# The down projection of a gated FFN: ten of its 21 blocks of rows go in pairs through seven products of blocks in place of eight

## The chip, the cores and the metric

The kernel runs on one core of one Trainium2 chip. The metric is the device time of one execution in microseconds (us), of which smaller is better; several executions are timed, and one more is profiled.

## The reference

One decoder layer for 512 tokens of 1024 channels in float32: a token mixer (pooling and sparse attention) and then an FFN. Only the FFN matters here; `D_FF` is 2752 and the convolution has three taps.

```
def conv_ffn(h, w_up, conv_w, conv_b, w_down):
    u = h @ w_up                                   # (512, 1024) @ (1024, 5504)
    up = jnp.pad(u, ((0, 0), (CONV_WIDTH - 1, 0), (0, 0)))
    c = conv_b + conv_w[0] * up[:, 0:S]
    for tap in range(1, CONV_WIDTH):
        c = c + conv_w[tap] * up[:, tap:tap + S]
    gate, val = jnp.split(c, 2, axis=-1)
    return (jax.nn.silu(gate) * val) @ w_down      # (512, 2752) @ (2752, 1024)

h = rms_norm(x, ffn_norm_w[l])
x = x + conv_ffn(h, w_up[l], conv_w[l], conv_b[l], w_down[l])
```

## The kernel before

Everything lies transposed: channels on the 128 partitions, the 512 tokens along the free dimension. Each float32 operand of a product is split in two numbers of TensorE's format, `hi` and `lo` (the rest), and a product of two blocks is three matmuls: hi by hi, lo of the one by hi of the other, and the reverse (`mm3`, lines 105 to 111). ScalarE (ACT) writes `hi`, VectorE (DVE) then writes `lo` (`split`, lines 93 to 103).

Weights come through a ring (`Ring`, lines 148 to 164). SyncE (SP) issues one load for up to 1024 columns into one of two staging tiles `st`, and the load waits until DVE has written the `lo` of the staging tile's earlier content. ACT and DVE then split it into tiles of up to 512 columns, `hi` and `lo`, of which there are six each; a `split` waits until TensorE (PE) is through with the tile six back.

The FFN has two stages. The up projection makes 43 tiles of 128 channels (`conv_tile`, lines 831 to 839): 24 matmuls of 512 columns each, then the scaling by `rstdb`, the convolution on DVE and ACT, and for each pair of a gate and a value tile the product silu(gate) * value, which is split into `gh[j]` and `gl[j]`, j from 0 to 20. The last 64 of the 2752 rows stand in `gs`, high part on partitions 0 to 63 and low part on 64 to 127, so that two matmuls do their product.

The down projection (lines 859 to 880) goes over the eight blocks c of 128 output channels. For each there are three loads of 7 weight blocks (448 KB), 21 times three matmuls with the 512 tokens moving, two matmuls for `gs`, one addition of the residual `x1[c]` on DVE from PSUM, and the store. The eighth block is done in two halves of 256 tokens with a PSUM bank each. That is 7 x 65 matmuls of 512 columns and 130 of 256.

The order of the instructions on each engine is set by a scheduler when the kernel is built: the code gives the program's order, and the scheduler may put independent instructions of one engine in another order. On the chip each engine takes its own queue in order. PSUM has eight banks: six under the tag `m` and two under `g`.

Of the kernel before, what the change touches and what calls it, by code (L numbers as in the profile page):

```python
# [11 lines left out]
F32 = mybir.dt.float32  # L12
# [7 lines left out]
P = 128  # L20
S = 512
# [49 lines left out]
START = ((2, 2, 2, 2), (1, 1, 1, 1))  # L71
SS = (0, 0, 0, 0)
ST = (1, 1, 1)


@with_exitstack
def layer(ctx: ExitStack, tc: tile.TileContext, par, masks, xT, w_kva, w_tm, w_fm, w_pl, w_pbr,
          w_ab, w_o, w_up, w_dn, w_dl, cw1, cw2, outT):
    nc = tc.nc
    v, a, g, pe = nc.vector, nc.scalar, nc.gpsimd, nc.tensor  # L80
    cnt = [0]
# [49 lines left out]
    def bank(p, tag, name, bufs):  # L131
        return p.tile([P, S], F32, tag=tag, name=nm(name), bufs=bufs)
# [686 lines left out]


    fp = pool(ctx, "fp")
    gh = [fp.tile([P, S], F32R, name=f"gh{j}") for j in range(NG - 1)]
    gl = [fp.tile([P, S], F32R, name=f"gl{j}") for j in range(NG - 1)]
    gs = fp.tile([P, S], F32R, name="gs")
    wlh = fp.tile([P, 1024], F32R, name="wlh")
    wll = fp.tile([P, 1024], F32R, name="wll")
    conv = fp.tile([P, NFT, 4], F32, name="conv")
    nc.sync.dma_start(conv, par[:, NCONV:].rearrange("p (t c) -> p t c", c=4))

    def conv_tile(t):  # L830
# [6 lines left out]
        v.scalar_tensor_tensor(c[:, 2:], u[:, :S - 2], conv[:, t, 0:1], c[:, 2:], ALU.mult, ALU.add)  # L837
        return c

    for j in range(NG):  # L840
# [10 lines left out]
        a.activation(cg[:rows], cg[:rows], AF.Silu)  # L851
        v.tensor_tensor(cg[:rows], cg[:rows], cv[:rows], ALU.mult)
        if j == 0:
            split(gs[:64], gs[64:], cg[:64])
        else:
            split(gh[j - 1], gl[j - 1], cg)

    wls = wr.tile([P, 1024], F32, tag="st", name="wls", bufs=ring.bufs[0])
    for h in range(2):
        nc.sync.dma_start(wls[64 * h:64 * h + 64], w_dl)  # L860
    split(wlh, wll, wls)
    for c in range(8):
        sl = slice(c * P, (c + 1) * P)

        cols = [slice(0, S)] if c < 7 else [slice(h * S // 2, (h + 1) * S // 2) for h in range(2)]
        banks = [bank(psm, "m", "dn", 6) for _ in cols]
        ws = []
        for q_ in range(3):
            ws += ring(w_dn[c, :, q_ * 896:(q_ + 1) * 896], P, 7)
            if q_ < 2:  # L870
                for ps, cs in zip(banks, cols):
                    mm3(ps[:, cs], [(ws[k], (gh[k][:, cs], gl[k][:, cs])) for k in range(7 * q_, 7 * q_ + 7)],
                        first=q_ == 0, last=False)
        for ps, cs in zip(banks, cols):
            mm3(ps[:, cs], [(ws[k], (gh[k][:, cs], gl[k][:, cs])) for k in range(14, 21)], first=False, last=False)
            pe.matmul(ps[:, cs], wlh[:, sl], gs[:, cs], start=False, stop=False)
            pe.matmul(ps[:, cs], wll[:, sl], gs[:, cs], start=False, stop=True)
            o = fp.tile([P, S], F32, tag="o", name=nm("o"), bufs=2)
            v.tensor_tensor(o[:, cs], ps[:, cs], x1[c][:, cs], ALU.add)
            nc.sync.dma_start(outT[sl, cs], o[:, cs])  # L880


def _tables():
# [28 lines left out]
def _layout(inp):  # L912
# [18 lines left out]
    for j in range(21):  # L931
# [5 lines left out]

    w_in = one("w_in")
    dn = one("w_down")
    d = {  # L940
        "par": par,
        "masks": _masks(),
# [9 lines left out]
        "w_dn": tiles(dn[:2688]),  # L952
        "w_dl": dn[2688:],
        "cw1": np.stack([kmaj(w) for w in one("cmp_w1")]),
        "cw2": one("cmp_w2"),
    }
# [16 lines left out]
```

## Time and profile before

| | us |
|---|---|
| three timed runs | 836.55, 837.82, 837.59 |
| their median | 837.59 |
| the profiled execution, its time | 835.79 |
| its span, first to last instruction | 834.0 |
| first matmul of the down projection | 712.00 |
| last matmul of the down projection | 830.60 |

Of the profiled execution 1.8 us lie outside the span that the trace shows, and the median of the runs is 1.8 us above it.

A line of the trace names the program's line, the engine, the operation and the tiles (out<-in). `dn` is a PSUM bank of the down projection, `fm` one of the up projection. PEld is TensorE's weight load; a row of PE or PEld is longer than the distance between two of them, since they overlap in a pipeline.

### The profile page before, as it was taken

What the parts mean: (1) busy time and instruction counts of PE and PEld (TensorE: products, weight loads), DVE (VectorE), ACT (ScalarE), POOL (GpSimd) and SP (SyncE); (2) the same over time, 40 slices, a digit from 0 to 9 for tenths busy, and PEclk for the clock granted to TensorE, in tenths of its full rate; (3) what the DMA queues carried; (4) which work ended last, traced back from release to release, by engine and by line L of the source; (5) the groups of instructions that cost most, each with busy time, mean ns of one, the idle gap of its engine ahead of it and who ended that gap; (6) DMA issues with size and microseconds to landing.
All of it is one profiled execution on the core that took longest, in us unless ns stands there. A gap on an engine that the chain in (4) does not pass through costs nothing.

```text
span 834.0 us, 12146 instructions
## 1 busy us (share of the span) xinstructions
PE 814.9 (98%) x4291; PEld 694.2 (83%) x4291; DVE 558.1 (67%) x1178; ACT 457.2 (55%) x977; POOL 226.7 (27%) x308
## 2 busy tenths in 40 slices
PE   7999989999999999999999999999999999999998
PEld 6878979987878878788888888888888888888888
DVE  7598865778887878885555438877777776532321
ACT  6755766668777877884334436554544544322220
POOL 5687514357565765641001200000000000000000
PEclk9999999999999999999999999999999999999999
DMA  6443362550001100011443233322333333343430
GB/s 219 116 114 113 104 176 86 169 152 26 26 26 41 36 26 26 26 51 51 152 152 97 84 101 95 105 84 97 101 101 102 89 90 115 99 126 101 115 101 26
DMA packets 29861, 77.55 MB, mean 93 GB/s; under 512 B 5480, under 2 KB 10216, under 8 KB 29800
## 3 DMA queue, kind: packets, MB, share of 16 engines
q1 hardware_dynamic: 29800, 76.78, 30.7%
q8 instruction: 34, 0.56, 0.3%
q14 instruction: 27, 0.22, 0.1%
HBM read 69.94 MB, written 2.10 MB: 86 GB/s over the span
## 4 chain that ended last, share of the span: by engine, by line
PE 85%; DVE 8%; ACT 3%; POOL 2%; DMA 1%; issue 1%; SPq 0%; DVEq 0%; ACTq 0%; POOLq 0%
PE fm L111 16%; PE fm L110 16%; PE fm L109 16%; PE op L735 5%; PE dn L110 5%; PE dn L109 5%; PE dn L111 5%; PE tp L728 4%; PE ss L698 2%; PE ss L697 2%; PE tg L321 2%; PE tg L320 2%; PE tg L319 2%; PE pb L109 1%; PE pb L110 1%
## 5 line engine op out<-in xcount | busy, mean ns | idle before, releaser
L97 ACT ACTIVATE hi<-st 128x512 fp32r<-128x512 f32 (+3 forms) x253 | 151.8, 607 | 192.5 <-PE fm L110 91.1
L100 DVE TENSOR_TENSOR lo<-st,hi 128x512 fp32r<-128x512 f32 (+1 forms) x210 | 142.6, 683 | 108.5 <-ACT hi L97 107.4
L109 PE MATMUL fm<-h2h,hi 128*128 128x512 f32 x344 | 133.9, 389 | 0.0
L110 PE MATMUL fm<-h2l,hi 128*128 128x512 f32 x344 | 133.8, 389 | 0.0
L111 PE MATMUL fm<-h2h,lo 128*128 128x512 f32 x344 | 133.7, 389 | 0.0
L709 POOL TENSOR_TENSOR pb<-pb,sm 128x128 f32<-128x128 f32 (+3 forms) x128 | 91.3, 745 | 51.1 <-DVE sm L706 28.0
L687 ACT ACTIVATE pb<-pb,nm 128x384 f32<-128x384 f32 (+3 forms) x128 | 70.9, 554 | 11.9 <-DVE nm L686 10.9
L109 PEld LDWEIGHTS fm<-h2h,hi 128*128 128x128 f32 x344 | 64.6, 188 | 13.5
L110 PEld LDWEIGHTS fm<-h2l,hi 128*128 128x128 f32 x344 | 64.6, 188 | 13.3
L111 PEld LDWEIGHTS fm<-h2h,lo 128*128 128x128 f32 x344 | 64.6, 188 | 13.3
L109 PE MATMUL fm<-hh,hi 128*128 128x512 f32 x160 | 71.1, 444 | 0.0
L111 PE MATMUL dn<-gh,lo 128*128 128x512 f32 (+1 forms) x189 | 69.1, 365 | 0.0
L110 PE MATMUL dn<-gl,hi 128*128 128x512 f32 (+1 forms) x189 | 69.1, 365 | 0.0
L109 PE MATMUL dn<-gh,hi 128*128 128x512 f32 (+1 forms) x189 | 69.1, 365 | 0.0
L686 DVE CUSTOM_DVE_ANT_0 pb<-ss,mk 128x384 f32<-128x384 f32 (+3 forms) x128 | 58.8, 485 | 14.5 <-PE ss L698 10.2
L111 PE MATMUL fm<-hh,lo 128*128 128x512 f32 x160 | 63.3, 396 | 0.7 <-POOL lo L100 0.7
L100 DVE TENSOR_TENSOR ptl<-tp,pth 128x512 fp32r<-128x512 f32 (+1 forms) x96 | 56.6, 594 | 10.8 <-ACT pth L97 10.3
L110 PE MATMUL fm<-hl,hi 128*128 128x512 f32 x160 | 63.0, 394 | 0.0
L97 ACT ACTIVATE pth<-tp 128x512 fp32r<-128x512 f32 (+1 forms) x96 | 49.3, 517 | 24.3 <-PE tp L728 24.1
L100 POOL TENSOR_TENSOR lo<-st,hi 128x512 fp32r<-128x512 f32 x36 | 47.8, 1333 | 37.5 <-ACT hi L97 32.6
L319 PE MATMUL tg<-hi,hh 128*128 128x256 f32 x192 | 54.1, 285 | 0.0
L320 PE MATMUL tg<-hi,hl 128*128 128x256 f32 x192 | 54.0, 285 | 0.0
(256 smaller groups left out, 1788.8 us busy)
## 6 DMA issues: line engine op xcount, KB each, us to landing
st<-in_w_up SPq DMA_DIRECT2D x43, 512.0 KB, 3.5
st<-in_w_dn SPq DMA_DIRECT2D x24, 448.0 KB, 3.7
st<-in_w_fm SPq DMA_DIRECT2D x20, 512.0 KB, 3.5
st<-in_w_tm SPq DMA_DIRECT2D x12, 512.0 KB, 3.6
qp<-qs SPq DMA_DIRECT2D x32, 128.0 KB, 2.6
st<-in_w_ab SPq DMA_DIRECT2D x8, 512.0 KB, 3.5
st<-in_w_o SPq DMA_DIRECT2D x8, 512.0 KB, 3.5
x<-in_xT SPq DMA_DIRECT2D x15, 256.0 KB, 5.1
```

The costliest lines, as they stand in the source:

```text
L97: a.activation(hi, src, AF.Copy)
L100: (eng or v).tensor_tensor(lo, src, r32(hi), ALU.subtract)
L109: pe.matmul(ps, sh, mh_, start=first and i == 0, stop=False)
L110: pe.matmul(ps, sh, ml_, start=False, stop=False)
L111: pe.matmul(ps, sl, mh_, start=False, stop=last and i == n - 1)
L319: pe.matmul(ps[:, :n], hh[k][:, tt], H, start=k == 0, stop=False)
L320: pe.matmul(ps[:, :n], hl[k][:, tt], H, start=False, stop=False)
L686: v.tensor_tensor_reduce(p_, ps, mcaus[:, S - n:], -1.0, 3e38, ALU.add, ALU.min, nm_[:, i:i + 1])
L687: a.activation(p_, p_, AF.Exp, bias=nm_[:, i:i + 1], scale=-1.0, accum_out=sm[:, i:i + 1])
L709: g.tensor_tensor(pb[:, PBASE[i]:PBASE[i] + n], pb[:, PBASE[i]:PBASE[i] + n], sm[:, i:i + 1].to_broadcast([P, n]), ALU.mult)
L728: last = pe.transpose(tp[:, n:n + P], pb[:, PBASE[i] + j * P:PBASE[i] + (j + 1) * P], ident)
L735: pe.matmul(op[:, j * P:], V2[b][j][:, G], pt_[:, TBASE[j]:TBASE[j] + w], start=b == 0 and j == 0 and part == 0, stop=False)
```

## The change

The last 11 blocks of rows and the 64 rows at the end stay as they were. The first ten go in five pairs p. The output channels go in four groups m of two blocks, so that a pair and a group have four weight blocks, and the tokens go in two halves of 256. The 2 x 2 x 2 products of blocks with 256 columns are replaced by seven products (the form of Strassen's scheme that is due to Winograd): sums of the activations are made in the up projection (`sums`), sums of the weights when they are loaded (`weights7`), and the seven products accumulate over the five pairs in four banks, of which `bb` and `bd` also take the 11 ordinary blocks.

- Activations: for a pair, the two products silu * value stand in `R` (128 x 1024). GpSimd (POOL) makes four differences of 128x256 in `T`, and ACT and DVE split 768 columns of `R` and the 1024 of `T` into `Bh[p]`, `Bl[p]`. For the last eight blocks the product is kept unsplit in `gw`, and its split is made in group 0 of the down projection, into the tiles of `h2h` and `h2l`, which are free after the last matmul of the up projection.
- Weights: a load of four blocks (256 KB) into `raw`, one of two staging tiles under the tag `rw`; one difference on POOL (line 906), three sums on DVE (lines 907 to 909), each 128x128; splits of 512 and of 384 columns through the ring's tiles. The ordinary blocks come in loads of 256 KB through the ring.
- In a group the steps alternate: c0 (an ordinary block for both output blocks, six matmuls of 512 columns), s0 (a pair, 21 matmuls of 256 columns), c1, s1, and so on to s4, then c5 to c11.
- After s4 the partial sums of `ba` and `bc` are combined on ACT and DVE and added to the residual; after c11 `bb` and `bd` are added, and `x1` itself is stored. In group 3 the second block's addition and store go in two halves.

```diff
+NSP = 5
+    NCB = NG - 1 - 2 * NSP
+    NEB = NCB - KC
+    def sums(jb, cg, cv):
+        if jb % 2 == 0:
+            raws[0] = [fp.tile([P, 4, 256], F32, tag="rw", name=nm("rw"), bufs=2) for _ in range(2)]
+        R, T = raws[0]
+        e = 2 * (jb % 2)
+        v.tensor_tensor(R[:, e:e + 2].rearrange("p k c -> p (k c)"), cg, cv, ALU.mult)
+        if jb % 2:
+            p = jb // 2
+            g.tensor_tensor(T[:, 0], R[:, 0], R[:, 1], ALU.subtract)
+            g.tensor_tensor(T[:, 1], R[:, 2], R[:, 0], ALU.subtract)
+            g.tensor_tensor(T[:, 2], R[:, 2], T[:, 0], ALU.subtract)
+            g.tensor_tensor(T[:, 3], R[:, 3], T[:, 2], ALU.subtract)
+            split(Bh[p][:, :3], Bl[p][:, :3], R[:, 1:4])
+            split(Bh[p][:, 3:], Bl[p][:, 3:], T)
...
+    def m256(ps, sa, k, p, first, done):
+        for n_, (w_, b_) in enumerate(((0, Bh), (0, Bl), (1, Bh))):
+            last = pe.matmul(ps, sa[w_], b_[p][:, k], start=first and n_ == 0, stop=done and n_ == 2)
+        return last
+    def weights7(m, p):
+        raw = fp.tile([P, 8, P], F32, tag="rw", name=nm("raw"), bufs=2)
+        nc.sync.dma_start(raw[:, 0:4], w_ds[m, p].rearrange("p (k c) -> p k c", c=P))
+        g.tensor_tensor(raw[:, 4], raw[:, 1], raw[:, 0], ALU.subtract)
+        v.tensor_tensor(raw[:, 5], raw[:, 0], raw[:, 3], ALU.add)
+        v.tensor_tensor(raw[:, 6], raw[:, 3], raw[:, 4], ALU.subtract)
+        v.tensor_tensor(raw[:, 7], raw[:, 2], raw[:, 6], ALU.subtract)
+        res = []
+        for o, n in ((1, 4), (5, 3)):
+            hi, lo = (wr.tile([P, 512], F32R, tag=t_, name=nm(t_), bufs=ring.bufs[1])[:, :n * P]
+                      .rearrange("p (k c) -> p k c", c=P) for t_ in ("hi", "lo"))
+            split(hi, lo, raw[:, o:o + n])
+            res += [(hi[:, k], lo[:, k]) for k in range(n)]
+        return res
...
-    for c in range(8):
...
-                    mm3(ps[:, cs], [(ws[k], (gh[k][:, cs], gl[k][:, cs])) for k in range(7 * q_, 7 * q_ + 7)],
...
+    for m in range(4):
...
+        for kind, i in order:
+            if kind == "c":
+                if m == 0 and NEB <= i < NCB:
+                    split(gh[i], gl[i], gw[i - NEB])
+                if i % 2 == 0:
+                    n = min(2, NCB + 1 - i)
+                    cload = ring(w_dc[m, :, i * 256:(i + n) * 256], P, 2 * n)
...
+            A11, A12, A22, S3, S1, S2, S4 = weights7(m, i)
+            for ps, hf, A, k, new in ((ba, 0, A11, 0, True), (bb, 1, A12, 2, False), (bd, 1, A22, 6, False),
+                                      (bc, 1, S3, 4, True), (bc, 0, S1, 3, False), (ba, 1, S2, 5, False),
+                                      (bb, 0, S4, 1, False)):
...
+        for e, (ps, x_) in enumerate(((bb, x1a), (bd, x1b))):
+            c = 2 * m + e
+            for cs in H if end and e else [slice(0, S)]:
+                v.tensor_tensor(x_[:, cs], ps[:, cs], x_[:, cs], ALU.add)
+                nc.sync.dma_start(outT[c * P:(c + 1) * P, cs], x_[:, cs])
```

Up to the first matmul of the down projection the queue of PE is the same in both kernels. In the down projection PE had, for a block of rows, three matmuls of 512 columns with the weights moving on by one block each time (here the first output block of those that follow the first two):

```order
L109 MATMUL dn_7895<-gh_5792,hi_7898 128x512
L110 MATMUL dn_7895<-gl_5813,hi_7898 128x512
L111 MATMUL dn_7895<-gh_5792,lo_7899 128x512
L109 MATMUL dn_7895<-gh_5793,hi_7898 128x512
L110 MATMUL dn_7895<-gl_5814,hi_7898 128x512
```

Now it has, at the end of c4 and the start of s4 in group 1 (`dn_8018` to `dn_8021` are bb, bd, ba, bc of that group; `hi_8216`, `lo_8217` are the first four weight blocks of s4):

```order
L940 MATMUL dn_8019<-gh_7689,hi_8200 128x512
L940 MATMUL dn_8019<-gl_7690,hi_8200 128x512
L940 MATMUL dn_8019<-gh_7689,lo_8201 128x512
L899 MATMUL dn_8020<-Bh_5812,hi_8216 128x256
L899 MATMUL dn_8020<-Bl_5817,hi_8216 128x256
L899 MATMUL dn_8020<-Bh_5812,lo_8217 128x256
```

Each product of a pair is three matmuls of 256 columns, and the third needs the `lo` that DVE writes.

DVE's queue in the down projection was low parts of weights in the order of their use, with one addition for each output block:

```order
L100 TENSOR_TENSOR lo_7831<-st_7828,hi_7830 128x512
L100 TENSOR_TENSOR lo_7835<-st_7828,hi_7834 128x384
L100 TENSOR_TENSOR lo_7862<-st_7859,hi_7861 128x512
L100 TENSOR_TENSOR lo_7866<-st_7859,hi_7865 128x384
L879 TENSOR_TENSOR o_7793<-dn_7697,x_0_5404 128x512
L100 TENSOR_TENSOR lo_7899<-st_7896,hi_7898 128x512
```

Now DVE has, in the middle of group 1 (`raw_8122`, `raw_8163` and `raw_8210` hold the weights of s2, s3 and s4 of this group, `raw_8333` those of s0 of the next):

```order
L101 TENSOR_TENSOR lo_8129<-raw_8122,hi_8128 128x512
L101 TENSOR_TENSOR lo_8133<-raw_8122,hi_8132 128x384
L101 TENSOR_TENSOR lo_8170<-raw_8163,hi_8169 128x512
L907 TENSOR_TENSOR raw_8210<-raw_8210 128x128
L101 TENSOR_TENSOR lo_8174<-raw_8163,hi_8173 128x384
L908 TENSOR_TENSOR raw_8210<-raw_8210 128x128
L909 TENSOR_TENSOR raw_8210<-raw_8210 128x128
L101 TENSOR_TENSOR lo_8201<-st_8198,hi_8200 128x512
L907 TENSOR_TENSOR raw_8333<-raw_8333 128x128
L908 TENSOR_TENSOR raw_8333<-raw_8333 128x128
L909 TENSOR_TENSOR raw_8333<-raw_8333 128x128
L101 TENSOR_TENSOR lo_8217<-raw_8210,hi_8216 128x512
```

The sums of a later load stand ahead of the low parts of an earlier one: the three sums on `raw_8333` ahead of `lo_8217` of s4.

SP's queue had three loads and a store for each output block:

```order
L155 DMA st_8057<-in_w_dn 128x896
L155 DMA st_8094<-in_w_dn 128x896
L155 DMA st_8125<-in_w_dn 128x896
L880 DMA out<-o_7991 128x512
L155 DMA st_8156<-in_w_dn 128x896
```

Now it has, in the same part of group 1, the loads of both kinds and the two stores of group 0:

```order
L905 DMA raw_8122<-in_w_ds 128x512
L905 DMA raw_8163<-in_w_ds 128x512
L970 DMA out<-x_0_5404 128x512
L970 DMA out<-x_1_5405 128x512
L156 DMA st_8261<-in_w_dc 128x512
L905 DMA raw_8210<-in_w_ds 128x512
L905 DMA raw_8333<-in_w_ds 128x512
L156 DMA st_8279<-in_w_dc 128x512
```

A load into `raw` waits until DVE has written the second low part (384 columns) of the load two back, and whatever stands behind it in SP's queue waits with it.

## Rows read from the trace of the kernel before

**Rows 1.** The page's first part: busy us of each engine, share, instructions.
```profile
PE 814.9 (98%) x4291; PEld 694.2 (83%) x4291; DVE 558.1 (67%) x1178; ACT 457.2 (55%) x977; POOL 226.7 (27%) x308
```

**Rows 2.** Busy time by stage: end of up, and down projection (PEclk: granted TensorE clock).
```profile
core 0: us, PE busy (x) PEld busy (x) DVE busy (x) ACT busy (x) POOL busy (x), PEclk, DMA share, GB/s
600.00:712.00 112.00, 112.00 (x496) 92.75 (x495) 83.20 (x124) 54.98 (x83) 0.00 (x0) 1.00 0.34 98
712.00:834.00 122.00, 118.88 (x586) 100.97 (x584) 35.56 (x58) 26.51 (x46) 0.00 (x0) 1.00 0.33 96
```

**Rows 3.** The chain of work that ended last, 712 to 834, by line.
```profile
by line: PE dn L110 31.4%; PE dn L109 31.4%; PE dn L111 31.4%; PE dn L877 1.5%; PE dn L876 1.5%; DVE o L879 0.3%; PE fm L111 0.2%; issue 0.0%
```

**Rows 4.** Who waited for whom, 720 to 834: us in total, times, longest.
```profile
ACT hi L97 <- PE dn L110: 74.3, 40, 2.6
```

**Rows 5.** Timeline: the down projection's first and last matmuls, last addition, last store.
```profile
712.00 0.39 PE L109 MATMUL dn<-gh,hi 128*128 128x512 f32 x1
...
815.13 0.28 PE L109 MATMUL dn<-gh,hi 128*128 128x256 f32 x1
...
830.60 0.28 PE L877 MATMUL dn<-gs,wll 128*128 128x256 f32 x1
830.92 0.42 DVE L879 TENSOR_TENSOR o<-dn,x 128x256 f32<-128x256 f32 x1 [2.33 <-PE dn L877]
831.37 0.33 SPq L880 DMA_DIRECT2D out<-o  x1
```

**Rows 6.** Groups by form, 720 to 834: busy us, mean ns | idle before.
```profile
L109 PEld LDWEIGHTS dn<-gh,hi 128*128 128x128 f32 x177 | 33.4, 189 | 5.3
...
L100 DVE TENSOR_TENSOR lo<-st,hi 128x512 fp32r<-128x512 f32 x20 | 13.9, 693 | 43.9 <-ACT hi L97 43.9
L97 ACT ACTIVATE hi<-st 128x512 fp32r<-128x512 f32 x20 | 12.6, 632 | 46.1 <-PE dn L110 46.1
...
L100 DVE TENSOR_TENSOR lo<-st,hi 128x384 fp32r<-128x384 f32 x20 | 11.2, 558 | 24.7 <-ACT hi L97 24.7
```

**Rows 7.** Groups by form, whole span: the small additions and POOL's.
```profile
L686 DVE CUSTOM_DVE_ANT_0 pb<-ss,mk 128x128 f32<-128x128 f32 x32 | 9.1, 286 | 4.2 <-PE tp L728 2.7 <-DMA qp<-qs 0.8
...
L300 POOL TENSOR_TENSOR h<-h,T 128x128 f32<-128x128 f32 x32 | 16.4, 533 | 47.0 <-issue 30.7 <-ACT h L293 15.1 <-DVE hrs L305 0.8
...
L100 POOL TENSOR_TENSOR hi<-st,hi 128x256 fp32r<-128x256 f32 x8 | 6.8, 848 | 4.7 <-ACT hi L97 4.7
```

**Rows 8.** DMA issues (KB each, us to landing) at 713.5 and at 428.7, and their starts.
```profile
st<-in_w_dn SPq DMA_DIRECT2D x1, 448.0 KB, 3.2
...
st<-in_w_o SPq DMA_DIRECT2D x1, 512.0 KB, 3.5
x<-in_xT SPq DMA_DIRECT2D x1, 256.0 KB, 3.6
...
428.72 0.33 SPq L155 DMA_DIRECT2D st<-in_w_o  x1
429.32 0.33 SPq L810 DMA_DIRECT2D x<-in_xT  x1
```

**Rows 9.** Timeline: POOL behind ACT at 445; DVE behind PE at 449.
```profile
445.07 0.62 ACT L212 ACTIVATE sq<-x 128x512 f32<-128x512 f32 x1
445.82 1.29 POOL L213 TENSOR_TENSOR ssum<-ssum,sq 128x512 f32<-128x512 f32 x1 [66.88 <-ACT sq L212]
...
448.73 0.39 PE L111 MATMUL fm<-mh,lo 128*128 128x512 f32 x1
...
449.16 0.69 DVE L813 TENSOR_TENSOR x<-fm,x 128x512 f32<-128x512 f32 x1 [1.49 <-PE fm L111]
```

**Rows 10.** Timeline from 21.4: DVE and POOL at work at the same time.
```profile
21.47 1.56 DVE L100 TENSOR_TENSOR lo<-st,hi 128x512 fp32r<-128x512 f32 x2 [0.42 <-ACT hi L97]
...
21.59 1.77 POOL L277 TENSOR_TENSOR C<-pl__110 128x128 f32<-128x128 f32 x2
```

More of the change, by code (lines that the diff above doesn't have):

```diff
@@ L821, in layer @@
     fp = pool(ctx, "fp")
[L822 to L823 removed]
+    NCB = NG - 1 - 2 * NSP
+    NEB = NCB - KC
+    gh = [fp.tile([P, S], F32R, name=f"gh{j}") for j in range(NEB)]
+    gl = [fp.tile([P, S], F32R, name=f"gl{j}") for j in range(NEB)]
+    gw = [fp.tile([P, S], F32, name=f"gw{j}") for j in range(KC)]
     gs = fp.tile([P, S], F32R, name="gs")
[L825 to L826 removed]
+    fp.tile([P, 48], F32, name="fpad")
+    Bh = [fp.tile([P, 7, 256], F32R, name=f"Bh{p}") for p in range(NSP)]
+    Bl = [fp.tile([P, 7, 256], F32R, name=f"Bl{p}") for p in range(NSP)]
     conv = fp.tile([P, NFT, 4], F32, name="conv")
@@ L851, in layer @@
         a.activation(cg[:rows], cg[:rows], AF.Silu)
+        if j and j <= 2 * NSP:
+            sums(j - 1, cg, cv)
+            continue
+        k = j - 1 - 2 * NSP
+        if j and k >= NEB:
+            v.tensor_tensor(gw[k - NEB], cg, cv, ALU.mult)
+            continue
         v.tensor_tensor(cg[:rows], cg[:rows], cv[:rows], ALU.mult)
@@ L855, in layer @@
         else:
[L856 to L861, printed above, removed]
-    for c in range(8):
[L863 to L871, printed above, removed]
-                    mm3(ps[:, cs], [(ws[k], (gh[k][:, cs], gl[k][:, cs])) for k in range(7 * q_, 7 * q_ + 7)],
[L873 to L880, printed above, removed]
@@ new lines, in layer @@
+            split(gh[k], gl[k], cg)
+    for k in range(KC):
+        gh.append(xp.tile([P, S], F32R, tag=f"hh{k}", name=f"gh{NEB + k}"))
+        gl.append(xp.tile([P, S], F32R, tag=f"hl{k}", name=f"gl{NEB + k}"))
+    def m256(ps, sa, k, p, first, done):
[16 more added lines that the diff above has]
+        return res
@@ L939, in _layout @@
     dn = one("w_down")
+    blk = lambda k, c: dn[k * P:(k + 1) * P, c * P:(c + 1) * P]
+    ds = np.stack([np.stack([np.concatenate([blk(2 * p, 2 * m + 1), blk(2 * p, 2 * m), blk(2 * p + 1, 2 * m),
+                                             blk(2 * p + 1, 2 * m + 1)], axis=1) for p in range(NSP)])
+                   for m in range(4)])
+    rem = np.concatenate([dn[2688:], dn[2688:]])
+    dc = np.stack([np.concatenate([blk(k, c) for k in range(2 * NSP, 21) for c in (2 * m, 2 * m + 1)]
+                                  + [rem[:, 2 * m * P:(2 * m + 2) * P]], axis=1) for m in range(4)])
     d = {
@@ L951, in _layout @@
         "w_up": tiles(one("w_up")[:, cols]),
-        "w_dn": tiles(dn[:2688]),
-        "w_dl": dn[2688:],
+        "w_ds": ds,
+        "w_dc": dc,
         "cw1": np.stack([kmaj(w) for w in one("cmp_w1")]),
```

36 lines of the change are left out of this document (35 added, 1 removed).

## The prediction

> **What bounds the kernel now.** I read the page's first part to find the engine, then the busy time by stage, the chain that ended last, the waits, and the timeline at the down projection's two ends. TensorE is busy 98% of the span [rows 1]. In the last 112 us of the up projection it is busy without a gap, at a granted clock of 1.00 (2.4 GHz), and in the down projection for 118.88 of 122 us [rows 2]. The chain there is TensorE's own matmuls in sequence, with 0.3% for the last addition [rows 3]. The other engines wait for it: ACT stood 74.3 us for matmuls to give its tiles back [rows 4], and DVE is busy for only 35.56 of the 122 us [rows 2]. So time is saved only by a shorter matmul stream, and lost where a weight's `lo` comes later than the stream asks for it.
>
> The distance of two matmuls comes out of the starts [rows 5]. From 712.00 to 815.13 there are 7 x 65 = 455 of 512 columns: 226.7 ns each. From 815.13 to 830.60 there are 129 steps of 256 columns: 119.9 ns. A matmul of half the columns thus costs 53%, not 50%.
>
> **The matmuls.** Before: 455 x 0.2267 + 130 x 0.1199 = 118.7 us. After, for each of four groups: 11 blocks x 6 + 4 for the last rows = 70 matmuls of 512 columns, and 5 pairs x 7 products x 3 = 105 of 256. In all 280 x 0.2267 + 420 x 0.1199 = 63.5 + 50.4 = 113.8 us, for 700 matmuls in place of 585. The stream is 4.9 us shorter. Two parts make it up: a pair of blocks in a group falls from 12 x 0.2267 = 2.72 us to 21 x 0.1199 = 2.52 us, twenty times, which is 4.0 us, and the eighth block is no longer done in halves, 0.9 us.
>
> The Trainium skill (TensorE: Matmul & The Clock Gate, "Back-to-back issue gap") puts the gap at columns / 2.4 GHz + 2.5 ns, which makes 215.8 and 109.2 ns. By that estimate the stream would go from 112.4 to 106.3 us and save 6.1 us. This trace has about 13 ns over the array's time in either size, not 2.5, and more matmuls pay it more often.
>
> **The end.** Before, DVE began the last addition 0.32 us after the last matmul's start, took 0.42 us, and the span ended 2.63 us after the store's issue at 831.37 [rows 5]. After, the last four matmuls of 512 columns are two for bb, then two for bd. DVE begins an addition 0.43 us behind the start of a last matmul of 512 columns [rows 9]. So with t the start of bd's last, bb's 512 columns are added from t - 0.02 to t + 0.67 (0.69 us, as the row of 128x512 [rows 6]), then come bd's two halves, 0.42 us each, to t + 1.51. The store is issued 0.8 us later than before, counted from the last matmul's start. That start itself stands 0.2267 instead of 0.1199 us before the stream's end, which gives 0.1 back; two more stores in flight may take it again. I count +0.8.
>
> **What is added beside the stream.** In the up projection, each pair costs POOL four differences of 128x256 (848 ns by its nearest row [rows 7], 3.4 us), and ACT and DVE split 1792 columns in place of 1024, some 1 us more each; 16 instructions of splits for the last eight blocks leave the stage. Five pairs add about 5 us to DVE and the eight blocks take 8 x 0.69 = 5.5 us off it, in a stage where it has 29 of 112 us free [rows 2]. The ring's six tiles, three tiles of the projection ahead, are the cover. Without it a pair could hold ACT for POOL's 3.4 us, five times; I count nothing.
>
> In a group of the down projection DVE has six low parts of ordinary loads, and for each of five pairs three sums and two low parts: 6 x 0.69 + 5 x (3 x 0.29 + 0.69 + 0.56) = 14.7 us [rows 6, 7], and some 4.5 us of additions at the group's end, under the 28.5 us of its matmuls. In group 0 the eight splits that were moved add 5.5 us: still under. So no engine's sum is the bound. What matters is latency.
>
> **The wait to look at.** Of the weights for pairs only two loads fit into the `raw` tiles, and DVE's queue strings them: the low part of s4 stands behind the three sums on the next group's first load, which can't be issued before s3's second low part has freed its tile, which stands behind a sum on s4's load, and so on back. Between the low part that frees a tile at the start of a group and the first low part of s4, four loads of landing time L follow each other:
> - load of s2, then POOL (0.13 to reach it [rows 9], 0.53 [rows 7]) and two sums of 0.29 on DVE with hand-offs, 1.3 in all, then 0.56 for a low part of 384 columns: L + 1.9;
> - load of s3, the same 1.3, then low parts of 512 and 384 of s2: L + 2.6;
> - load of s4, one sum and a low part of 384: L + 0.9;
> - load of the next group's s0, 1.3, then 0.69: L + 2.0.
>
> Hand-offs from DVE to the load's issue (0.03 as in [rows 5]) included, this is 4 L + 7.4. TensorE asks for that low part 17.1 us into the group: four times 6 x 0.2267 + 21 x 0.1199, then c4 and two more. I walked the queues of the changed kernel on paper from the first matmul of the stage, each instruction with the duration of its row, starting when its engine, its inputs and its buffer allow. At L = 2.75 the string begins 3.5 us ahead of group 1, 2.6 ahead of group 2, 2.3 ahead of group 3 (whose s4 has no further load behind it); each 0.1 us on L takes about 0.4 off the lead.
>
> **How long is L?** No row shows a lone load of 256 KB. Bounds: 448 KB took 3.2 and 512 KB 3.5 us [rows 8], a line that goes down to 2.3 us; and 3.6 us for 256 KB that went out 0.60 us behind 512 KB. That pair gives the value that I take: the first landed at 428.72 + 3.5 = 432.22, the second at 429.32 + 3.6 = 432.92, so 256 KB moved in 0.7 us, 512 KB move in 1.4, the rest is 2.1, and L = 2.1 + 0.7 = 2.8 us. Then group 2, the tightest, has 17.1 + 2.4 - (4 x 2.8 + 7.4) = 0.9 us to spare. The margin is gone at L = 2.9; the walk gives stalls of 4.4 us in all at 3.2 and 9.2 us at 3.5.
>
> At the change of stage the last tiles of the up projection, seven moved low parts and c2's weights share DVE; in the walk c2's low part is ready 2 us before it is asked for, since c0, s0, c1 and s1 (7.8 us) run on weights made earlier.
>
> **The sum,** against the profiled execution: -4.9 + 0.8, and 0.3 for a small stall that the thin margin makes likely: 834.0 - 3.8 = 830.2 us of span, 832.0 with the 1.8 us outside. The median of the runs is 1.8 us above the profiled one, so I carry the difference over: 837.59 - 3.8 = 833.8 us. A measurement of this kernel tells about 0.2% (1.7 us) from no change.
>
> **Rivals.**
> 1. *The pairs' loads come late* (the other side). Two loads of 256 KB are often out together, with the ordinary loads and stores among them, and then L is nearer to 3.6 than to 2.8. At L = 3.5 the 9.2 us of stalls make 833.5 + 9.2 = 842.7 us, slower; the stalls eat the gain at L = 3.2, and the verdict is slower from 3.3. For it: the string has 0.9 us of slack, and DVE's order can't overlap the loads. Against: the transfers take 0.7 us each, and one string has one of them out at a time.
> 2. *DVE and POOL slow each other.* POOL's difference and DVE's first sum start on the same landing. While both worked, two low parts of 512 columns took 1.56 us and two POOL steps of 128x128 1.77 us [rows 10], against 0.69 and 0.53 apart. POOL's step then takes 0.89 and the string is 3 x 0.36 = 1.1 us longer: the margin of 0.9 is gone, and the walk gives 0.5 us of stalls at L = 2.8 and 2 at 2.9. Alone: 834 to 835.5 us, still faster. The Trainium skill says the same against this change (GPSIMD Engine Reference, "1. Specifications"): POOL's way into SBUF is shared with VectorE and contended when a DVE instruction has two inputs there, as all of these sums have. Rows 10 agree.
> 3. *The weight loads bound the short matmuls.* A weight load is 189 ns by its row [rows 6], the same for either size. Were it not overlapped, 420 x (0.189 - 0.120) = 29 us would be added: 862 us. Against it stand 129 steps at 119.9 ns with the same weight loads [rows 5].
> 4. *Half of the gain is lost at the change of stage:* if DVE's moved splits come 2 to 4 us late there, 835.8 to 837.8 us, no difference. For it: TensorE waits there for ACT and DVE at once, and only the walk speaks against it.
>
> **How the numbers follow.** The forecast, with 2 or the like inside it (stalls up to 2.4 us, below 835.9): 0.66. Stalls of 2.4 to 5.8 us, from 1 at L between 3.1 and 3.3 or from 4: 0.15, no difference. Stalls above that, rival 1: 0.17. Rival 3: 0.02. So faster 0.66, same 0.15, slower 0.19. The range begins at the full gain with a smaller tail, 832.6, and goes up into the middle of rival 1, 841.0 (stalls of 7.5 us). It leaves out the pages' larger gain and the worse half of rival 1. The likeliest case's own range is 832.6 to 835.9.
>
> **What would show it.** In the new trace: 512 columns at 227 and 256 columns at 120 ns; 700 matmuls in some 114 us from the first; loads of `raw` that land 2.7 to 2.9 us after issue; DVE's sums in the sequence above, and TensorE waiting, if at all, for low parts of s4 in groups 1 and 2 and of s2 in group 3, not for ACT. I am wrong if those loads take over 3.1 us, if 256 columns run slower among 512, or if the first group stalls.

## The result, and the profile after

| | before | after |
|---|---|---|
| timed runs, median (lowest to highest) | 837.59 us (836.48 to 837.99) | 832.29 us (830.73 to 834.19) |
| ratio after to before, 95% interval | | 0.9944 (0.9929 to 0.9959) |
| span of the profiled execution | 834.0 | 831.3 |
| first matmul of the down projection to the end of the span | 122.0 | 117.4 |
| of it: to the start of the last matmul | 118.60 | 112.70 |
| of it: from there to the end | 3.40 | 4.67 |

The changed kernel is faster: 5.3 us by the medians, 4.7 by the ratio (by its interval 3.4 to 5.9). In the profiled executions the down projection is 4.6 us shorter: its stream of matmuls 5.9 shorter, its end 1.3 longer.

The spans differ by 2.7 us only, because the down projection begins later, at 713.93 instead of 712.00. The up projection is not the cause: from its first matmul to the first of the down projection it is 235.84 us in both (476.16 to 712.00, 478.09 to 713.93). Most of the 1.93 us is the granted clock in the mixer: the matmul that begins at 59.98 in the kernel before begins at 60.34 in the changed one, 0.36 later, and the one at 79.94 begins at 81.82, 1.87 later. Here are the stretch from 60 to 80 us of the kernel before, then that of the changed one (columns as in [rows 2]):

```profile
60.00:80.00 20.00, 17.97 (x141) 17.33 (x140) 17.32 (x33) 10.52 (x28) 14.58 (x22) 1.00 0.32 99
```

```profile
60.00:80.00 20.00, 17.97 (x127) 17.29 (x127) 16.98 (x33) 10.89 (x29) 14.59 (x22) 0.91 0.33 97
```

TensorE was busy for 17.97 of the 20 us both times, and once it got 0.91: from 76 to 78 us its clock was 0.50, 1.2 GHz, in the changed kernel, and 1.00, 2.4 GHz, in the kernel before. From 70 to 75 us it had been busy for 2.97 us in both, so its work there doesn't tell the two apart. Of the five timed runs of the changed kernel one has a mean clock of 1.000 and a span of 828.9, two 0.997 (830.1, 830.5), two 0.995 (831.3, 831.7): some 1.3 us for each such drop. So the stage alone is compared below, from its first matmul to the end.

The page's first line of the changed kernel, then the busy time by stage:

```profile
PE 810.7 (98%) x4406; PEld 696.6 (84%) x4406; DVE 599.4 (72%) x1277; ACT 468.2 (56%) x996; POOL 256.1 (31%) x348
```

```profile
600.00:712.00 112.00, 112.00 (x496) 92.78 (x495) 83.49 (x128) 53.55 (x80) 3.65 (x5) 1.00 0.31 94
714.00:826.00 112.00, 112.00 (x698) 101.25 (x697) 69.95 (x151) 37.40 (x67) 9.54 (x17) 1.00 0.35 104
```

TensorE has no gap in the down projection either, though DVE is now busy for 70 of 112 us there instead of 36 of 122 [rows 2]. Who waited for whom, over the whole stage of the changed kernel (us in total, times, longest):

```profile
POOL raw L906 <- DMA raw<-in_w_ds: 83.7, 15, 9.8
DVE raw L907 <- DMA raw<-in_w_ds: 21.7, 14, 2.5
...
ACT hi L98 <- PE dn L899: 18.0, 16, 2.3
ACT hi L98 <- PE dn L940: 14.9, 11, 2.6
```

No line has PE on its left side. ACT's waits for tiles fell from 74.3 us [rows 4] to 33; DVE's for loads are new.

The timeline at the first ordinary block and the first pair (L940 has the ordinary blocks, L899 the pairs):

```profile
713.93 0.39 PE L940 MATMUL dn<-gh,hi 128*128 128x512 f32 x1
...
715.29 0.28 PE L899 MATMUL dn<-Bh,hi 128*128 128x256 f32 x1
...
717.76 0.39 PE L940 MATMUL dn<-gh,hi 128*128 128x512 f32 x1
```

Six steps of 512 columns take 1.36 us, 226.7 ns each, as before. The 21 steps of 256 columns take 2.47 us, 117.6 ns each (117.7 as the mean over 400), not the 119.9 of [rows 5].

The loads of the stage (KB each, median us to landing):

```profile
st<-in_w_dc SPq DMA_DIRECT2D x21, 256.0 KB, 2.9
raw<-in_w_ds SPq DMA_DIRECT2D x17, 256.0 KB, 2.7
```

The landing times of all 20 loads into `raw`, of which three go out before the stage:

```profile
DMA to landing us min/median/max: 2.6/2.7/3.2
```

The place with least to spare, s4 of group 2: SP's issue of its load, the first of DVE's three sums on the load of the next group's s0, the low part of s4, and the matmul that asks for it:

```profile
777.11 4.17 SPq L905 DMA_DIRECT2D raw<-in_w_ds  x2
...
784.22 0.29 DVE L907 TENSOR_TENSOR raw<-raw 128x128 f32<-128x128 f32 x1 [2.20 <-DMA raw<-in_w_ds]
...
785.40 1.15 DVE L101 TENSOR_TENSOR lo<-raw,hi 128x512 fp32r<-128x512 f32 x2
...
787.32 0.28 PE L899 MATMUL dn<-Bh,lo 128*128 128x256 f32 x1
```

DVE stands for 2.20 us waiting for the load of s0 with the low part of s4 behind it in its queue. That load, issued at 780.95, is the one that took 3.2 us. The low part of 512 columns ends at 785.40 + 0.69 = 786.09, and is asked for at 787.32: 1.2 us to spare. Of the 20 first low parts of pairs this is the least; the others in groups 1 to 3 have 1.9 to 7.4.

The end (DVE's three additions; SP's issues of their stores, of which the last is the row at 828.24):

```profile
826.61 1.35 DVE L969 TENSOR_TENSOR x<-dn,x 128x512 f32<-128x512 f32 x3 [5.69 <-PE dn L940]
826.63 0.39 PE L940 MATMUL dn<-gs,lo 128*128 128x512 f32 x1
827.33 1.31 SPq L970 DMA_DIRECT2D out<-x  x3
...
828.24 0.40 SPq L970 DMA_DIRECT2D out<-x  x1
```

The additions end 1.33 us behind the last matmul's start, 826.61 + 1.35 = 827.96. The last store goes out only at 828.24, since SP's issues follow each other at 0.4 to 0.5 us, and the span ends 3.07 us behind that, instead of 2.63.

### The profile page after: what moved, and what is told of

It is laid out like the page before. It is cut to its first block, busy times and chain, and to the rows that moved or that the text cites. A ratio compares the mean times of both kernels' runs of the same rounds, so it can differ in the third digit from the quotient of the medians.

```text
span 831.3 us, 12631 instructions
## 1 busy us (share of the span) xinstructions
PE 810.7 (98%) x4406; PEld 696.6 (84%) x4406; DVE 599.4 (72%) x1277; ACT 468.2 (56%) x996; POOL 256.1 (31%) x348
## 4 chain that ended last, share of the span: by engine, by line
PE 84%; DVE 8%; DMA 2%; ACT 2%; POOL 2%; issue 1%; SPq 0%; DVEq 0%; ACTq 0%; POOLq 0%
PE fm L110 16%; PE fm L111 16%; PE fm L112 16%; PE dn L940 8%; PE dn L899 6%; PE op L736 5%; PE tp L729 4%; PE ss L699 2%; PE ss L698 2%; PE tg L322 2%; PE tg L321 2%; PE tg L320 2%; PE pb L110 1%; PE pb L112 1%; PE pb L111 1%
## 5 line engine op out<-in xcount | busy, mean ns | idle before, releaser
L98 ACT ACTIVATE hi<-st 128x512 fp32r<-128x512 f32 (+2 forms) x229 | 139.0, 614 | 156.1 <-PE fm L111 100.6
L101 DVE TENSOR_TENSOR lo<-st,hi 128x512 fp32r<-128x512 f32 (+1 forms) x186 | 133.0, 719 | 48.3 <-ACT hi L98 46.8
L906 POOL TENSOR_TENSOR raw<-raw 128x128 f32<-128x128 f32 x20 | 11.2, 561 | 196.7 <-DMA raw<-in_w_ds 190.3
L322 PE MATMUL tg<-lo,hh 128*128 128x256 f32 x192 | 54.3, 289 | 0.0
L729 PE MATMUL tp<-pk,pb 128*128 128x128 f32 x320 | 51.7, 274 | 1.4 <-DVE pc L661 1.2
```

What stands on the lines that cost most here:

```text
L98: a.activation(hi, src, AF.Copy)
L101: (eng or v).tensor_tensor(lo, src, r32(hi), ALU.subtract)
L322: pe.matmul(ps[:, :n], hh[k][:, tt], L, start=False, stop=k == KC - 1)
L729: last = pe.transpose(tp[:, n:n + P], pb[:, PBASE[i] + j * P:PBASE[i] + (j + 1) * P], ident)
```

## The experiments

### Why 256 columns came sooner: the order of the banks

In the kernel before, with its eighth block's halves mixed:

```diff
-                for ps, cs in zip(banks, cols):
-                    mm3(ps[:, cs], [(ws[k], (gh[k][:, cs], gl[k][:, cs])) for k in range(7 * q_, 7 * q_ + 7)],
-                        first=q_ == 0, last=False)
+                for k in range(7 * q_, 7 * q_ + 7):
+                    for ps, cs in zip(banks, cols):
+                        mm3(ps[:, cs], [(ws[k], (gh[k][:, cs], gl[k][:, cs]))], first=k == 0, last=False)
```

> The kernel before, with its eighth block's two halves taken alternately: three matmuls of 256 columns into the left half's bank, three into the right half's, and so on, in place of runs of 21 into one bank. In the changed kernel 256 columns took 117.7 ns from start to start, before 119.9. If runs into one bank are what costs the 2.2 ns, the 130 matmuls come at 117.7 ns here (15.3 us, 0.3 less). If it is the operands (the moving tile is the half of one of 512 columns in both forms here), they stay at 119.9. The span itself says little: the left half's addition of 0.42 us is no longer hidden, so 834.0 + 0.1 to 0.5 us at the clock of the run before.

```profile
820.07 0.28 PE L111 MATMUL dn<-gh,lo 128*128 128x256 f32 x1
...
820.91 0.28 PE L109 MATMUL dn<-gh,hi 128*128 128x256 f32 x1
```

Seven steps in 0.84 us, 120.0 ns each. So alternating the banks is not what makes it 117.7.

### Why 256 columns came sooner: where the operands lie

The change has one more line, which the diff shown further up leaves out: an unused tile of 48 columns (192 bytes) ahead of `Bh` and `Bl`. Three kernels without it, the second and third with an unused tile ahead of the first operands instead (16 and 8 columns):

```diff
     gs = fp.tile([P, S], F32R, name="gs")
-    fp.tile([P, 48], F32, name="fpad")
     Bh = [fp.tile([P, 7, 256], F32R, name=f"Bh{p}") for p in range(NSP)]
```

> The changed kernel without the unused tile of 48 columns that lies ahead of Bh and Bl, so that these begin 192 bytes earlier: at 96 bytes past a multiple of 128, as all operands of the 256-column matmuls at 119.9 ns did, in place of 32. If the place of the moving operand makes the difference, the 420 matmuls come at 120.0 ns in place of 117.7, and from the first matmul of the down projection to the start of the last it takes 112.7 + 420 x 0.0023 = 113.7 us, as forecast (113.6). If the shape of the tiles or the order of the banks makes it, the stream stays at 112.7.

> As the one before, and all operands of matmuls (activations, weights, sums) 64 bytes further: all of them begin 32 bytes past a multiple of 128. If the moving operand's own place counts, the 256 columns come at 117.7 ns again, and 512 columns perhaps 2.3 ns sooner than 226.7 as well: some 1500 matmuls of 512 columns in the two last stages and the mixer's, up to 3.5 us. If its place against the weights' counts, which is the same for all here as it was before the change, 256 columns come at 120.0 and 512 at 226.7.

> The same with all operands 32 bytes further, on multiples of 128 bytes. If a start on a multiple of 64 is what helps, both sizes come sooner than 117.7 and 226.7. If the place against the weights counts, 120.0 and 226.7.

The first of them, at the first pair and the ordinary block behind it:

```profile
714.64 0.28 PE L899 MATMUL dn<-Bh,hi 128*128 128x256 f32 x1
...
717.15 0.40 PE L940 MATMUL dn<-gh,hi 128*128 128x512 f32 x1
717.39 0.40 PE L940 MATMUL dn<-gl,hi 128*128 128x512 f32 x1
717.62 0.39 PE L940 MATMUL dn<-gh,lo 128*128 128x512 f32 x1
```

21 steps take 2.51 us in place of 2.47; all but the first are 120 ns. The first ordinary block behind a pair is slower too, 0.23 to 0.24 us a step. From the first matmul to the last start the stream is 114.04 us in all three kernels, 1.34 more than with the tile (20 x 0.04 = 0.8 of it for the pairs, the rest for the steps behind them). Moving everything together, by 64 or by 32 bytes, changed nothing: it is not the operands' own start that counts. What is left is the distance between the moving operand and the weights.

The next two runs have the weights alone 64 bytes further, in the changed kernel without its tile of 48 columns and in the kernel before. A second unused tile, left out below, has 240 columns (960 bytes) and brings the FFN's activations 1024 bytes further, to the same place modulo 512 bytes:

```diff
-    wr = pool(ctx, "wr")
+    wr = pool(ctx, "wr"); wr.tile([P, 16], F32, name="wpad")
```

> The changed kernel with no tile ahead of Bh and Bl, and with the weights' tiles alone 64 bytes further (the activations stand where the kernel before had them, 96 bytes past a multiple of 128, the weights at 32). In the last three runs 256 columns took 120.0 ns wherever all operands had been moved together, and 117.7 where the moving operand stood 192 bytes apart from the weights, modulo 1024. If a distance is enough, 420 matmuls take 117.7 ns again and the stream 112.7 us. For 512 columns two cases: 224.4 ns as well, then some 1500 matmuls of the two last stages, the projections and the mixer save up to 3.5 us, or 226.7 still, since their weight loads have more time. If it needs that one distance, 120.0 and 114.0.

> The kernel before with its weights' tiles 64 bytes further, its activations where they were. If the distance counts, its 130 matmuls of 256 columns take 117.7 in place of 120.0 (0.3 us less); if 512 columns gain too, the stream of the down projection is 118.60 - 1.3 = 117.3 us, else 118.3. If not, 118.6.

The changed kernel so shifted, in the up projection and at a pair:

```profile
690.12 0.40 PE L110 MATMUL fm<-h2h,hi 128*128 128x512 f32 x1
...
691.05 0.40 PE L111 MATMUL fm<-h2l,hi 128*128 128x512 f32 x1
```

```profile
726.18 0.28 PE L899 MATMUL dn<-Bh,hi 128*128 128x256 f32 x1
...
726.89 0.28 PE L899 MATMUL dn<-Bh,hi 128*128 128x256 f32 x1
```

256 columns take 118 ns again (six steps in 0.71 us), so a distance of its own is enough for them. In the kernel before, so shifted, the steps of 256 columns take 117.8 ns too, in tiles of 512 columns. 512 columns, which I had expected to gain or stay, are slower: four steps in 0.93 us, 233 ns. The up projection takes 242.57 us in both shifted kernels in place of 235.84, the down projection's stream 114.44 instead of 112.70, and 121.32 instead of 118.60. With one run each the times were 842.05 and 847.01 us. So, of the places tried, 512 columns are quickest with the moving operand and the weights at the same place modulo 512 bytes (the distance of two weight blocks), 256 columns with the two apart. The changed kernel has just that, by its 192 bytes. Besides the same place only two distances were tried, 192 bytes and -64, and these are the same modulo 256: the period is not shown, and neither are 512 columns at 192.

The place does not settle the step alone: two of the runs on the string of loads, further down, have steps of 113 ns at the addresses of 117.7.

### The eighth block in 512 columns

In the kernel before:

```diff
-        cols = [slice(0, S)] if c < 7 else [slice(h * S // 2, (h + 1) * S // 2) for h in range(2)]
+        cols = [slice(0, S)]
```

> The kernel before, with the eighth block in 512 columns like the others. The stream from the first matmul of the down projection to the last start was 118.60 us; with 65 x 0.2267 in place of 130 x 0.1199 it is 117.6 by the forecast's prices. The end grows: DVE starts 0.43 instead of 0.32 us behind the last matmul's start, takes 0.69 instead of 0.42, and a store of 256 KB takes some 0.3 longer than one of 128 KB: from the last start to the end 4.1 us in place of 3.40. So the stage is 121.7 us in place of 122.0: of the 0.9 us that the forecast counts for the halves, 0.3 remain. A rival, that the end costs nothing more: 121.0.

```profile
830.90 0.39 PE L877 MATMUL dn<-gs,wll 128*128 128x512 f32 x1
831.32 0.69 DVE L879 TENSOR_TENSOR o<-dn,x 128x512 f32<-128x512 f32 x1 [13.70 <-PE dn L877]
832.04 0.34 SPq L880 DMA_DIRECT2D out<-o  x1
```

The stream is 117.64, the end 4.00 (the store's issue to the end 2.85), the stage 121.64 us: as expected. Of the 0.96 us that whole blocks save in the stream, 0.37 remain; the halves were worth 0.6 at the end.

### The string of loads

POOL's difference four times over:

```diff
-        g.tensor_tensor(raw[:, 4], raw[:, 1], raw[:, 0], ALU.subtract)
+        for _ in range(4):
+            g.tensor_tensor(raw[:, 4], raw[:, 1], raw[:, 0], ALU.subtract)
```

> The changed kernel, with POOL's difference on each load of weights for a pair made four times over (the same result, three times 0.55 us more in each load's step). The theory of the string: four loads, their sums and low parts follow each other, group 2's s4 had 1.2 us of lead, so 1.65 us on each of three or four steps uses it up. The walk over this kernel's queues at a landing time of 2.72 us gives 6.3 us of waits of TensorE, 2.7 of them each in groups 2 and 3 and 0.5 to 1 in group 1, all at the first low part of s2 or s4. Rival: TensorE's stream has far more cover than the string says (it did not wait once), and the stage stays within 1 us of 117.4.

TensorE's waits (PE and PEld are the same wait, seen at the matmul and at its weight load), the engines' busy time and the clock over three stretches, and the longest wait, at s2 of group 2:

```profile
PEld dn L899 <- DVE lo L101: 6.7, 4, 3.1
...
PE dn L899 <- DVE lo L101: 5.8, 4, 2.9
```

```profile
714.00:776.00 62.00, 59.99 (x376) 53.98 (x375) 42.19 (x85) 21.37 (x39) 23.85 (x38) 1.00 0.33 103
776.00:792.00 16.00, 13.12 (x71) 11.72 (x70) 7.99 (x19) 3.87 (x7) 5.72 (x12) 0.79 0.37 113
792.00:835.60 43.60, 42.65 (x256) 37.87 (x254) 24.31 (x51) 11.47 (x22) 10.85 (x20) 1.00 0.27 80
```

```profile
781.51 2.17 POOL L906 TENSOR_TENSOR raw<-raw 128x128 f32<-128x128 f32 x4 [4.14 <-DMA raw<-in_w_ds]
...
783.92 0.69 DVE L101 TENSOR_TENSOR lo<-raw,hi 128x512 fp32r<-128x512 f32 x1
...
784.65 0.58 PE L899 MATMUL dn<-Bh,lo 128*128 128x256 f32 x1 [2.88 <-DVE lo L101]
```

The stream takes 122.31 us, 9.6 more. The waits stand at s2 of group 1 (1.8 us), s4 of group 1 (0.5), s2 of group 2 (3.0) and s2 of group 3 (1.1): 6.5 in all, where the walk gave 6.3, though it gave group 3 more and group 1 less. Nearly all of the remaining 3.1 us is the clock's: around the longest wait 16 us got 0.79, and 16 x 0.21 = 3.4, a part of it within the wait. Behind that wait, from 785.04 to 788.66, TensorE ran at 1.2 GHz, and 17 steps of 256 columns took 213 ns each. So the string is real. The clock fell only at the wait of 3.0 us: with the waits of 1.8 and 0.5 us ahead of it and of 1.1 us behind it the stretches stand at 1.00.

The second run on the string changes only how the weights lie in DRAM, in pieces of 512 bytes:

```diff
-        nc.sync.dma_start(raw[:, 0:4], w_ds[m, p].rearrange("p (k c) -> p k c", c=P))
+        nc.sync.dma_start(raw[:, 0:4], w_ds[m, p].rearrange("k p c -> p k c"))
```

> The changed kernel, with the weights for pairs lying in DRAM so that each load of 256 KB is made of pieces of 512 bytes in place of 2 KB. The order of every queue is the same. If the pieces make the landing time L longer, the string's price shows: no wait up to 2.9 us, 3.8 us of waits at 3.2, 7.8 at 3.5, at s4 of groups 1 and 2 and s2 of groups 2 and 3. If L stays at 2.7, the stage stays at 117.4 us. Rival: the loads are hidden anyway, and a longer L moves nothing.

```profile
raw<-in_w_ds SPq DMA_DIRECT2D x16, 256.0 KB, 2.8
```

The median L grew by only 0.1 us, and the stage stayed at 117.47 us (a single run of 831.20). What the string had to spare fell, in group 2's s4 from 1.2 to 0.6 us and in group 3's s2 from 1.9 to nothing: a first wait of 0.04 us shows there, 805.19 to 805.35. One load made it, that of s3 in group 3, issued at 799.28, whose sums stand ahead of the low part of s2 in DVE's queue:

```profile
raw<-in_w_ds SPq DMA_DIRECT2D x1, 256.0 KB, 4.0
```

```profile
803.43 0.29 DVE L907 TENSOR_TENSOR raw<-raw 128x128 f32<-128x128 f32 x1 [2.41 <-DMA raw<-in_w_ds]
```

That the smaller pieces made this load late is not shown: in the kernel without the unused tile, whose pieces are of 2 KB, a load issued at 780.70 took 4.8 us and left s4 of group 2 only 0.2 us. Neither the price of a common L of 3.2 nor a margin used up at 2.9 is therefore measured; the string is as late as its latest load.

Behind this short wait TensorE's steps in the same pair are shorter than anywhere in the changed kernel:

```profile
806.16 0.28 PE L899 MATMUL dn<-Bh,lo 128*128 128x256 f32 x1
...
806.84 0.28 PE L899 MATMUL dn<-Bh,lo 128*128 128x256 f32 x1
```

Six steps take 0.68 us, 113 ns each, with every operand where it was at 117.7 ns. The pair as a whole is no shorter (2.55 us), since one step behind the wait took 0.22 us. In the run with POOL's difference four times over 113 ns came too, in two pairs behind their waits and in the pair behind the stretch at 1.2 GHz, but not behind the wait in group 3. Why is open.

### Fewer pairs

```diff
-NSP = 5
+NSP = 3
```

> The changed kernel with three pairs in place of five (six blocks of rows in pairs, 15 ordinary ones). A pair in a group takes 21 x 0.1177 = 2.47 us in place of 12 x 0.2267 = 2.72, so two pairs fewer in four groups cost 8 x 0.25 = 2.0 us: the stream 114.7, the stage 119.4 us, with the end as it was and without waits. By the forecast's price for 256 columns (119.9 ns) it would be 1.6 us more, 119.0. If pairs cost something beside the matmuls, as in contention of the loads or the sums, it shows as less than 2.0.

The stream is 114.68 and the stage 119.35 us, 1.97 more than with five pairs, with the end at 4.67 and no wait. A pair is thus worth 0.25 us in each group and costs nothing else here.

### A shorter end

First with bd's halves in one bank: the last two steps of group 3 go first for bb, then for bd's left and right half.

```diff
+                if end and i == NCB - 1:
+                    continue
+                tail = end and i == NCB
-                for e, ps in enumerate((bb, bd)):
+                for e, ps, cs in ((0, bb, slice(0, S)), (1, bd, H[0]), (1, bd, H[1])) if tail else \
+                        ((0, bb, slice(0, S)), (1, bd, slice(0, S))):
+                    for k in (i - 1, i) if tail else (i,):
...
```

> The changed kernel with the last two steps of group 3 in another order: first both blocks for bb, then bd in two halves of 256 columns (10 matmuls in place of 5). bb's addition and store and the left half's lie beside matmuls, as the left half's did before the change. From the last matmul's start to the end 3.4 us as before the change, in place of 4.67; the stream gets 0.07 longer and its last start is 0.1 later: the stage 116.3 in place of 117.4, 1.1 less, and a ratio of 0.992 to 0.9935 to the kernel before. Rival: the end is bound by the store's landing, whichever additions stand ahead, and nothing or up to 0.4 us is gained.

```profile
825.50 0.28 PE L945 MATMUL dn<-gs,lo 128*128 128x256 f32 x1
825.82 0.76 DVE L974 TENSOR_TENSOR x<-dn,x 128x256 f32<-128x256 f32 x2 [0.50 <-PE dn L945]
```

DVE had been free for 0.50 us and took both halves only 0.32 us behind the right half's last matmul: the row shows one wait ahead of both, for the later one. The end is 4.14, the stage 117.01 us: 0.4 gained, not 1.1, which is what the rival allowed, and not my sum. The median is 831.19, the ratio 0.9937 (0.9919 to 0.9955).

Then with a bank for each half, and bd closed and added after c9:

```diff
+                if end and i == NCB - 1:
+                    v.tensor_tensor(x1b, bd, x1b, ALU.add)
+                    continue
+                tail = end and i == NCB
+                parts = ((0, bb, 0), (1, bd, 0))
+                if tail:
+                    hb = bank(psm, "m", "dn", 6), bank(psm, "m", "dn", 6)
+                    parts = (0, bb, 0), (1, hb[0][:, H[0]], H[0]), (1, hb[1][:, H[1]], H[1])
...
```

> The changed kernel with another end for group 3: bd is closed after c9 and added to the residual beside matmuls; then the last two steps for bb, then for bd's left and right half in a bank each (10 matmuls of 256 columns), so that only the right half's addition is left behind the last matmul. In the run before this, where both halves stood in one bank, DVE began the left one only after the right one's last matmul, and the end was 4.14 us. With a bank each: 0.32 to DVE's start, 0.42 of addition, and 2.6 to 2.9 from the store's issue to the end, 3.4 to 3.7 us from the last matmul's start; the stream 112.9; the stage 116.3 to 116.6 us in place of 117.4, and a ratio of 0.992 to 0.9935. Rival: the end stays at 4.1 because three stores are under way, stage 117.0.

```profile
826.31 0.28 PE L949 MATMUL dn<-gs,lo 128*128 128x256 f32 x1
...
826.62 0.42 DVE L980 TENSOR_TENSOR x<-dn,x 128x256 f32<-128x256 f32 x1 [0.17 <-PE dn L949]
...
827.08 0.41 SPq L981 DMA_DIRECT2D out<-x  x1
```

The right half alone is left behind the last matmul. The end is 3.76 us, of which 2.99 from the store's issue, with two stores issued shortly before; before it was 2.63. The stage is 116.63 us, 0.75 less than the changed kernel's. The median is 831.48, the ratio 0.9935 (0.9913 to 0.9957): better than the kernel before for certain, and better than the changed kernel by the trace only, since 0.1% is less than the runs can tell.

## Why the prediction was right, and where its sum was off

The direction and the mechanism were right: TensorE's stream was the bound, the stream got shorter, and the rest was hidden. The forecast was 833.8 us. The median of the runs is 832.3, 0.3 below the low end of the range, and 837.59 times the ratio 0.9944 is 832.9, 0.3 above it: the result stands at the edge of the range. Term by term, in the stage:

| term | forecast | measured |
|---|---|---|
| matmuls (first start to last start, and the last one's step) | -4.9 | 118.72 to 112.93: -5.8 |
| the end, from the stream's end | +0.8 | +1.2 (4.67 - 0.23 against 3.40 - 0.12) |
| waits | +0.3 | 0 |
| sum | -3.8 | -4.6 |

The misses have both signs, -0.9, +0.4 and -0.3, and add up to -0.8.

**The matmuls.** The mis-sized term is the step of 256 columns. I took 119.9 ns from the only run of them in the down projection, as if columns alone set it. The place of the operand does too, and the change has a line for that, which I left out of the diff and out of the sum: without the tile of 48 columns the stream was 114.04 us, and my price gives 113.6 to the last start. The line was worth 1.3 us. By an estimate from the formula of the Trainium skill (TensorE: Matmul & The Clock Gate, "Back-to-back issue gap"), which the page gives for an isolated matmul, the saving would have been 6.1 us, nearer in total to what came. The trace doesn't agree with its reason: a step has 11 ns over the columns' time at 256 columns and 13 at 512 here, not 2.5 at both. The two parts of the term can now be told apart: the eighth block undone alone saves 0.96 in the stream, and twenty pairs save 20 x 0.25 = 5.0.

**The end.** The additions were done sooner than I wrote (1.33 us behind the last matmul's start, not 1.51, since each begins some 0.08 us before the one ahead of it is over). What I had put aside with "may take it again" was the larger part: SP's issues of the three stores are 0.4 to 0.5 us apart, and from the last store's issue to the end of the span it is 3.07 us with two others under way instead of 2.63. The run with a bank for each half moves all but one addition away and still shows 2.99. That the other stores are the cause is argued, not shown.

**Beside the stream.** The up projection, with the sums on POOL and longer splits, took 235.84 us as before; nothing was the right count. Rival 4 fell: TensorE did not wait at the change of stage.

**The wait to look at.** The median L was 2.7 (forecast 2.8), the tightest place was s4 of group 2, with 1.2 us to spare (forecast 0.9 at 2.8, and 0.4 us for each 0.1). The string showed itself when it was made longer, with 6.5 us of waits. The walk gave all loads one L, and that is not how they came: one took 3.2 us, above the 3.1 named as a sign of being wrong, and TensorE did not wait for it. In the kernels with the same queues, which differ from it by unused tiles or by how the weights lie in DRAM, single loads took up to 4.8 us, and the least that was spare ran from nothing to 3.0 us (none in the run with pieces of 512 bytes, 0.2 in the kernel without the tile, 3.0 in the one with everything 64 bytes further). So rival 1 is a true mechanism, and that it cost nothing in the profiled execution is in part luck. The 0.3 us for a small stall were not needed.

**Rival 2** came about, though not where it was looked for, and it was hidden. The groups by form in the down projection of the changed kernel, then POOL's step at s4 of group 2 with what DVE did beside it, and the longest of POOL's steps:

```profile
L906 POOL TENSOR_TENSOR raw<-raw 128x128 f32<-128x128 f32 x17 | 9.5, 561 | 90.1 <-DMA raw<-in_w_ds 83.7 <-DVE lo L101 5.2 <-DVE raw L909 1.2
L907 DVE TENSOR_TENSOR raw<-raw 128x128 f32<-128x128 f32 x17 | 5.0, 292 | 21.7 <-DMA raw<-in_w_ds 21.7
```

```profile
779.93 0.55 POOL L906 TENSOR_TENSOR raw<-raw 128x128 f32<-128x128 f32 x1 [4.61 <-DMA raw<-in_w_ds]
780.07 0.81 DVE L101 TENSOR_TENSOR lo<-raw,hi 128x384 fp32r<-128x384 f32 x1
...
717.80 1.23 POOL L906 TENSOR_TENSOR raw<-raw 128x128 f32<-128x128 f32 x1 [7.46 <-DMA raw<-in_w_ds]
```

POOL's step and DVE's first sum start on the same landing and hardly slow each other: 561 ns against 533 in [rows 7], not the 890 worked out from [rows 10], and 292 against 286. The low part that DVE starts next, while POOL is at work, is the one that pays. Seven low parts of the stage began within a POOL step, and the four of 512 columns took 0.95 us in place of 0.69, the three of 384 columns 0.81 to 0.82 in place of 0.56 [rows 6]. Once it was POOL's turn, at 717.80, behind a low part of DVE that had just begun, and it took 1.23 us. So the string of group 2 pays 0.26 us once, at 780.07, not 0.36 three times, and that is within what it had to spare. **Rival 3** fell with 117.7 ns.

Not settled: the medians differ by 5.3 us, the ratio gives 4.7, the stages differ by 4.6. The interval holds all three, and the drops of the clock in the mixer, 1.3 us each and in differing number from run to run, are enough for the difference. That the kernels differ in their number was not shown. The forecast of the profiled execution alone, 830.2 us of span, fell short by 1.1 us, though its stage was 0.8 shorter than forecast: the later start of the stage is the rest.

## What to carry to other kernels

Read every line of a change for what it does to the addresses, an unused tile too: a step's price, as measured here, holds for the size and for the place of its operands, and even so a wait just before can change it. When a shorter stream leaves DVE's queue in an order in which sums on a later load stand ahead of an earlier low part, compute the string of loads and what it has to spare, with the latest load of a trace and not with the median; it decides between a gain and a loss long before any engine is full. And at a kernel's end count the issues of all stores that go out together and the time from the last one to the end, not the additions alone.

## What the runs showed of the hardware

- The time from the start of one matmul to the next went with where the moving operand lies against the weights, taken modulo 512 bytes. At the same place, 256 columns took 120.0 ns and 512 columns 226.7; with the moving operand 192 bytes further, 256 took 117.7; with it 64 bytes back, 256 took 118 and 512 took 233. Moving both by 32 or 64 bytes changed neither. Why is open; other distances were not tried, and the two that were are the same modulo 256.
- At one and the same place 256 columns took 117.7 ns in the changed kernel and 113 behind a wait of 0.04 us in the run with pieces of 512 bytes.
- An ordinary block of 512 columns behind a run of 120.0 ns steps also took 231 to 236 ns for some of its steps, and 226.7 behind a run of 117.7 ns.
- A wait of TensorE of 3.0 us went with a granted clock of 0.79 over the 16 us around it, a part of them at 1.2 GHz, which cost about as much again. Waits of 1.8, 0.5 and 1.1 us in the same execution left the clock at 1.00.
- The pairs' loads of 256 KB took 2.6 to 3.2 us to land in the changed kernel, and 2.4 to 4.8 in the one without its unused tile.
- With POOL's subtraction of 128x128 running when they began, DVE's subtractions took 0.95 us at 512 columns and 0.81 to 0.82 at 384, in place of 0.69 and 0.56. POOL's own took 1.23 us where one of DVE's had begun at the same time, and 0.47 to 0.55 otherwise.
- Three stores issued one behind the other went out 0.4 to 0.5 us apart, and the span ended 3.0 us after the last one's issue, where with a single one of the same 128 KB it ended after 2.63.
